# Hybrid backbone block on one core: one operand's low part by a VectorE subtraction, four weight sums on GpSimd

## The chip, the cores and the metric

The kernel runs on one core of a Trainium2 chip. The metric is the device time of one execution in microseconds (us), lower is better. Every execution computes both layers of the model from inputs in device memory. A difference of 0.2% (5.4 us) is about what repeated measurements of this kernel can tell from none.

## The reference

Two layers over 256 latent tokens and 256 context tokens of width 1024, all in fp32. Each layer is a half-step SwiGLU feed-forward network (FFN), a mixer with three branches, and a second FFN; each is modulated by a conditioning vector and closed by a layer norm. What matters here is the FFN, for the latent tokens `x` and the context tokens `xc` with the same weights:

```python
def swiglu(u, w1, w3, w2):
    return (jax.nn.silu(u @ w1) * (u @ w3)) @ w2

def ffn_sublayer(h, mod, w1, w3, w2, g, b):
    u = h * (1 + mod[1]) + mod[0]
    return layer_norm(ALPHA * h + 0.5 * mod[2] * swiglu(u, w1, w3, w2), g, b)

x = ffn_sublayer(x, ada_x[0], ffn_w1[l, 0], ffn_w3[l, 0], ffn_w2[l, 0], ...)
xc = ffn_sublayer(xc, ada_c[0], ffn_w1[l, 0], ffn_w3[l, 0], ffn_w2[l, 0], ...)
```

The hidden width is 2816, that is 22 tiles of 128 columns (`ft` 0 to 21).

## The kernel before

**Precision.** An fp32 product is made of three fp32r matmuls: every operand is split into a high part (a copy to fp32r on ScalarE, ACT) and a low part (operand minus high part, a subtraction on VectorE, DVE), and high x high, high x low and low x high are added up in PSUM. `split_into` (L228 to L230) writes such a pair for a weight or an activation, `wchunk` (L181) loads one weight tile of 512 KB into a buffer `raw` and splits it (L189, L190).

**Block products.** In the second FFN of layer 0 and the first of layer 1, hidden tiles 4 to 21 (18 in each, 36 in all) take the two weights' products with both token streams from seven block products instead of eight. `wquads` (L193) makes the weight side of one tile: it loads `r1` and `r3` (w1 and w3, L202), each with two halves of 512 columns for the two halves of the contraction, and makes four pairs:

- `a` (wahi, walo) from `r1`;
- `d` (wdhi, wdlo) from the second half of `r3`;
- then four sums of halves, written in place over `r3` and `r1` (L214 to L217, each reading what the one before it wrote);
- `c` (wchi, wclo) from the new `r1`, `b` (wbhi, wblo) from the new `r3`.

The low part of `b` is made in another way than the rest: ACT copies `b`'s high part with a sign change into it (L223), and a DMA issued from the GpSimd (POOL) queue adds `r3` to that (L224, an accumulating DMA).

**Order on TensorE (PE).** `block` (L255) runs 12 matmuls of 256 columns for one product: 4 blocks of the contraction, three matmuls each (L263 high, L264 high, L265 low). `issue_after` chains the blocks, so that PE takes them in program order. For hidden tile n the order is: two blocks with a(n); one with d(n-1), the tile before (`x_blocks`); one with c(n) (`third_block`); one with c(n-1) (`ctx_blocks`); two with b(n) (`last_blocks`): seven blocks, 84 matmuls. Between the blocks small activation steps run on ACT and DVE (L575 to L608): L575, L588 and L594 copy a product out of PSUM on ACT, L583, L595, L601, L606 and L608 combine on DVE, L584 and L607 are SiLU, and `store` splits the result (gh, gl).

**Buffers.** Pool `wp` has five buffers each for `raw` (NR), high parts (`hi`) and low parts (`lo`, NW). A tile needs four pairs, and two pairs of the tile before are still in use, so a pair waits until an earlier one is read out. Weight preparation is issued at a higher priority than its place in the program (`tc.high_priority`, PRE = 140); the framework's scheduler sets the order on each engine from that.

**Around it.** The tiles come in groups of 3, 8 and 7 in each of the two FFNs; between the groups the down projection runs (w2ps, L242 to L244). In the background, DVE computes the conditioning (`ada_job`, L289 and L291, one multiply-add over 512 columns each); `tick` in `wquads` and `wchunk` lets it advance by a fixed rate per weight tile.

Of the kernel before, what the change touches and what calls it, by code (L numbers as in the profile page):

```python
# [8 lines left out]
F32 = mybir.dt.float32  # L9
F32R = mybir.dt.float32r  # L10
AF = mybir.ActivationFunctionType
ALU = mybir.AluOpType
# [39 lines left out]
def hybrid_kernel(tc, x, ctx, pos, cc, wada, pcol, w1, w3, w2a, w2b, wst, wv, wg, wbr, wout, dfc, dft, idn, lnrow, out):  # L52
    nc = tc.nc
# [11 lines left out]
    def nm(s):  # L65
        cnt[0] += 1
        return f"{s}_{cnt[0]}"
# [32 lines left out]
    act = nc.scalar.activation  # L100
    V = nc.vector
# [74 lines left out]
    def tick():  # L176
        debt[0] += rate[0]
        n = int(debt[0])
        debt[0] -= n
        bg(n)  # L180
# [12 lines left out]
    def wquads(src1, src3):  # L193


        tick()
        H = slice(0, 512), slice(512, 1024)
        with tc.high_priority(offset=PRE):
            raw = []
            for src in (src1, src3):  # L200
                t = wp.tile([P, 1024], F32, tag="raw", bufs=NR, name=nm("raw"))
                nc.sync.dma_start(out=t, in_=src)  # L202
                raw.append(t)
            r1, r3 = raw

            def halves(name, w=1024):
                return [wp.tile([P, 1024], F32R, tag=t, bufs=NW, name=nm(name + t))[:, :w] for t in ("hi", "lo")]

            a = halves("wa")
            split_into(a[0], a[1], r1)  # L210
            d = halves("wd", 512)
            split_into(d[0], d[1], r3[:, H[1]])
            add = dict(op=ALU.add)
            V.tensor_tensor(r3[:, H[1]], r3[:, H[0]], r3[:, H[1]], **add)  # L214
            V.tensor_tensor(r3[:, H[0]], r3[:, H[0]], r1[:, H[0]], **add)
            V.tensor_tensor(r1[:, H[0]], r3[:, H[1]], r1[:, H[0]], **add)
            V.tensor_tensor(r1[:, H[1]], r1[:, H[0]], r1[:, H[1]], **add)  # L217
            c = halves("wc")
            split_into(c[0], c[1], r1)

            b = halves("wb")
            act(b[0], r3, AF.Copy)
            act(b[1], b[0].bitcast(F32), AF.Copy, scale=-1.0)  # L223
            nc.gpsimd.dma_start(out=b[1].bitcast(F32), in_=r3, accum_op=ALU.add)  # L224

        return (a, 0), (a, 512), (d, 0), (b, 512), (c, 0), (b, 0), (c, 512)

    def split_into(h, l, src):  # L228
        first = act(h, src, AF.Copy)  # L229
        return first, V.tensor_tensor(l, src, h.bitcast(F32), op=ALU.subtract)  # L230
# [304 lines left out]
    def ffn(l, i, X, ys, T, nxt):  # L535
# [32 lines left out]
        def start_blocks(ft):  # L568

            f = dict(ft=ft, W=wquads(w1[l, i, ft], w3[l, i, ft]))  # L570
            f["r1"] = bank(mmp, "q1")[:, XR]
            f["c"], f["v"] = aslot("cc"), aslot("cv", 256)
            Q[:] = X.operands()
            block(f["r1"], f["W"][0], Q[0], True)
            act(f["c"][:, XR], f["r1"], AF.Copy)  # L575
            return f
# [539 lines left out]
    for part in range(4):  # L1116
# [4 lines left out]
        for kt in range(0, KT, 2):  # L1121
            raw = wp.tile([P, 1024], F32, tag="raw", bufs=NR, name=nm("araw"))
            for k in range(2):
                nc.sync.dma_start(out=raw[:, 512 * k:512 * k + 512].rearrange("p (v c) -> p v c", v=2),
                                  in_=wada[0, (kt + k) * P:(kt + k + 1) * P, 0:2 * D]
# [189 lines left out]
```

## Time and profile before

| | us |
|---|---|
| median of 3 runs (2713.5 to 2718.81) | 2718.05 |
| the profiled execution | 2721.58 |
| its span, first to last instruction | 2719.8 |
| TensorE matmuls busy | 2538.8 (93%) |
| VectorE busy | 1966.5 (72%) |
| ScalarE busy | 1109.8 (41%) |
| GpSimd busy | 80.5 (3%) |
| mean granted TensorE clock | 0.967 of full speed |

Matmuls are pipelined: a matmul's busy time overlaps the next one's, so the distance between two starts says what one costs. A row of a timeline gives start, duration, engine (SPq and the like are DMA queues), line, operation, output <- inputs, and in brackets how long the engine sat idle before it and what ended that.

### The profile page before, as it was taken

To read this page: it belongs to the slowest core of one execution; us is meant where nothing else is said; L and a number is where in the kernel's file an instruction comes from. 1 tells how busy PE (TensorE), PEld (TensorE's weight loads), DVE (VectorE), ACT (ScalarE), POOL (GpSimd) and SP (SyncE) were. 2 spreads that over 40 slices of the span, in tenths; PEclk is the share of its full clock that TensorE was granted. 3 is DMA by queue.
4 is the path that set the end of the run, shared out by engine and by line. 5 is a ranking of instruction groups with operands and counts; after the bars stand their busy time and mean duration, and the time that the engine had idled before them with its cause. 6 is when DMAs were issued, how large, how long until landed. Compare 5 with 4: busy or idle time off the path is not lost. (4 is left out here: it accounts for less than half of the span.)

```text
span 2719.8 us, 40624 instructions
## 1 busy us (share of the span) xinstructions
PE 2538.8 (93%) x15842; PEld 2231.9 (82%) x15842; DVE 1966.5 (72%) x3611; ACT 1109.8 (41%) x1834; POOL 80.5 (3%) x162
## 2 busy tenths in 40 slices
PE   8999999999999999998879799878889999999998
PEld 4777779788778888897767788777779888999998
DVE  5888887888777755587666568656556988987655
ACT  4222235333332324353442446343445334455543
POOL 0000000010100000000000000000000000000000
PEclk9999999999999999998889899988899999999999
DMA  9666663222133233326454444546353333556563
GB/s 287 197 207 191 190 199 108 90 67 89 59 102 96 67 128 97 120 86 170 111 130 133 115 132 133 146 132 178 106 142 99 106 116 119 176 166 210 159 197 125
DMA packets 135744, 372.99 MB, mean 137 GB/s; under 512 B 13313, under 2 KB 28929, under 8 KB 135553
## 3 DMA queue, kind: packets, MB, share of 16 engines
q1 hardware_dynamic: 130368, 351.53, 41.4%
q0 software_dynamic: 5184, 18.88, 3.7%
q8 instruction: 124, 2.03, 0.3%
q14 instruction: 68, 0.55, 0.1%
HBM read 344.11 MB, written 7.34 MB: 129 GB/s over the span
## 5 line engine op out<-in xcount | busy, mean ns | idle before, releaser
L189 ACT ACTIVATE whi<-raw 128x1024 fp32r<-128x1024 f32 (+1 forms) x426 | 444.1, 1044 | 872.6 <-issue 170.1
L190 DVE TENSOR_TENSOR wlo<-raw,whi 128x1024 fp32r<-128x1024 f32 (+1 forms) x426 | 511.5, 1202 | 278.7 <-ACT whi L189 275.6
L673 DVE SCALAR_TENSOR_TENSOR cy<-cz,dww,cy 128x482 f32<-128x482 f32 (+29 forms) x480 | 288.9, 602 | 17.4 <-ACT cy L765 10.5
L291 DVE SCALAR_TENSOR_TENSOR acc<-araw,sc,acc 128x512 f32<-128x512 f32 x392 | 275.1, 746 | 18.2 <-DMA araw<-in_wada_dram 17.3
L265 PE MATMUL q<-tH,wblo 128*128 128x256 f32 x288 | 109.5, 380 | 113.9 <-DMA wblo<-raw 113.9
L265 PEld LDWEIGHTS q<-tH,wblo 128*128 128x128 f32 x288 | 79.0, 274 | 122.5 <-DMA wblo<-raw 122.5
L242 PE MATMUL ffps<-op,whi 128*128 128x256 f32 x608 | 165.3, 281 | 3.9 <-ACT op L229 3.9
L243 PE MATMUL ffps<-op,whi 128*128 128x256 f32 x608 | 168.1, 280 | 0.0
L244 PE MATMUL ffps<-op,wlo 128*128 128x256 f32 x608 | 167.5, 279 | 0.0
L242 PE MATMUL ffps<-opH,whi 128*128 128x512 f32 x352 | 141.0, 403 | 0.7 <-ACT opH L229 0.7
L243 PE MATMUL ffps<-opL,whi 128*128 128x512 f32 x352 | 140.7, 400 | 0.0
L244 PE MATMUL ffps<-opH,wlo 128*128 128x512 f32 x352 | 140.1, 400 | 0.4 <-DVE wlo L190 0.4
L242 PE MATMUL w2ps<-gh,whi 128*128 128x512 f32 x336 | 134.2, 399 | 0.0
L244 PE MATMUL w2ps<-gh,wlo 128*128 128x512 f32 x336 | 133.5, 397 | 0.0
L243 PE MATMUL w2ps<-gl,whi 128*128 128x512 f32 x336 | 133.1, 396 | 0.0
L242 PE MATMUL mg<-opH,whi 128*128 128x512 f32 (+1 forms) x384 | 129.7, 338 | 0.0
L244 PE MATMUL mg<-opH,wlo 128*128 128x512 f32 (+1 forms) x384 | 129.5, 337 | 0.0
L243 PE MATMUL mg<-opL,whi 128*128 128x512 f32 (+1 forms) x384 | 129.4, 337 | 0.0
L242 PEld LDWEIGHTS ffps<-op,whi 128*128 128x128 f32 x608 | 113.0, 190 | 4.8 <-ACT op L229 4.3
L243 PEld LDWEIGHTS ffps<-op,whi 128*128 128x128 f32 x608 | 115.1, 190 | 0.2
L244 PEld LDWEIGHTS ffps<-op,wlo 128*128 128x128 f32 x608 | 114.8, 189 | 0.0
L263 PE MATMUL q<-tH,wbhi 128*128 128x256 f32 x288 | 102.7, 357 | 0.0
(390 smaller groups left out, 7358.0 us busy)
## 6 DMA issues: line engine op xcount, KB each, us to landing
raw<-in_w_dram SPq DMA_DIRECT2D x176, 512.0 KB, 4.1
raw<-in_wst_dram SPq DMA_DIRECT2D x144, 512.0 KB, 3.5
araw<-in_wada_dram SPq DMA_DIRECT2D x128, 512.0 KB, 4.2
raw<-in_w2b_dram SPq DMA_DIRECT2D x64, 512.0 KB, 4.2
raw<-in_wbr_dram SPq DMA_DIRECT2D x48, 512.0 KB, 3.5
wblo<-raw POOLq DMA_DIRECT2D x36, 512.0 KB, 5.3
raw<-in_w2a_dram SPq DMA_DIRECT2D x32, 384.0 KB, 3.2
araw<-in_wada_dram SPq DMA_DIRECT2D x32, 256.0 KB, 5.7
```

What stands on the lines that cost most here:

```text
L189: act(hi, raw, AF.Copy)
L190: V.tensor_tensor(lo, raw, hi.bitcast(F32), op=ALU.subtract)
L242: PE.matmul(ps, wh, xh, start=first and i == 0, stop=False)
L243: PE.matmul(ps, wh, xl, start=False, stop=False)
L244: PE.matmul(ps, wl, xh, start=False, stop=last and i == n - 1)
L263: PE.matmul(ps, wh, xh, start=first and k == 0, stop=False, **how)
L265: end = PE.matmul(ps, wl, xh, start=False, stop=k == 3, **how)
L291: V.scalar_tensor_tensor(accs[s], w, c, accs[s], op0=ALU.mult, op1=ALU.add)
L673: V.scalar_tensor_tensor(dv[:, :, a:b], sv[:, :, a + o:b + o], wcols[:, j:j + 1], dv[:, :, a:b], op0=ALU.mult, op1=ALU.add)
```

## The change

The four sums move from VectorE to GpSimd. The low part of `b` is made by `split_into`, like that of `a`, `c` and `d`: a subtraction on VectorE in place of ScalarE's sign-changed copy and the accumulating DMA. In the changed file the lines after `wquads` stand three lower: L229 and L230 are L226 and L227, L575 is L572, and so on.

```diff
             add = dict(op=ALU.add)
-            V.tensor_tensor(r3[:, H[1]], r3[:, H[0]], r3[:, H[1]], **add)
-            V.tensor_tensor(r3[:, H[0]], r3[:, H[0]], r1[:, H[0]], **add)
-            V.tensor_tensor(r1[:, H[0]], r3[:, H[1]], r1[:, H[0]], **add)
-            V.tensor_tensor(r1[:, H[1]], r1[:, H[0]], r1[:, H[1]], **add)
+            nc.gpsimd.tensor_tensor(r3[:, H[1]], r3[:, H[0]], r3[:, H[1]], **add)
+            nc.gpsimd.tensor_tensor(r3[:, H[0]], r3[:, H[0]], r1[:, H[0]], **add)
+            nc.gpsimd.tensor_tensor(r1[:, H[0]], r3[:, H[1]], r1[:, H[0]], **add)
+            nc.gpsimd.tensor_tensor(r1[:, H[1]], r1[:, H[0]], r1[:, H[1]], **add)
             c = halves("wc")
             split_into(c[0], c[1], r1)
-
             b = halves("wb")
-            act(b[0], r3, AF.Copy)
-            act(b[1], b[0].bitcast(F32), AF.Copy, scale=-1.0)
-            nc.gpsimd.dma_start(out=b[1].bitcast(F32), in_=r3, accum_op=ALU.add)
+            split_into(b[0], b[1], r3)
```

Where the scheduler puts the instructions. First ScalarE, between two evacuations of b's product (cv) in the middle of a group of tiles; before:

```order
L594 ACTIVATE cv_11554<-q_1832_11552 128x256
L229 ACTIVATE wchi_11671<-raw_11655 128x1024
L575 ACTIVATE cc_11681<-q_1849_11680 128x256
L222 ACTIVATE wbhi_11675<-raw_11657 128x1024
L584 ACTIVATE cc_11681<-cc_11681 128x256
L223 ACTIVATE wblo_11676<-wbhi_11675 128x1024
L229 ACTIVATE wahi_11802<-raw_11798 128x1024
L588 ACTIVATE cc_11681<-q_1849_11680 128x256
L229 ACTIVATE wdhi_11806<-raw_11800 128x512
```

and the same stretch of the changed kernel:

```order
L591 ACTIVATE cv_11546<-q_1832_11544 128x256
L226 ACTIVATE wchi_11663<-raw_11647 128x1024
L572 ACTIVATE cc_11672<-q_1849_11671 128x256
L226 ACTIVATE wbhi_11667<-raw_11649 128x1024
L581 ACTIVATE cc_11672<-cc_11672 128x256
L226 ACTIVATE wahi_11793<-raw_11789 128x1024
L585 ACTIVATE cc_11672<-q_1849_11671 128x256
L226 ACTIVATE wdhi_11797<-raw_11791 128x512
```

One copy of 1024 columns is gone; all else stands as it stood, wchi ahead of the copy of a's product (cc).

VectorE in the same stretch of the changed kernel, from one wclo to the last step before the next:

```order
L227 TENSOR_TENSOR wclo_11664<-raw_11647,wchi_11663 128x1024
L580 TENSOR_TENSOR cc_11672<-q_1852_11687,cc_11672 128x256
L227 TENSOR_TENSOR wblo_11668<-raw_11649,wbhi_11667 128x1024
L598 SCALAR_TENSOR_TENSOR cc_11545<-q_1832_11544,cc_11545 128x256
L227 TENSOR_TENSOR walo_11794<-raw_11789,wahi_11793 128x1024
L603 TENSOR_TENSOR cc_11545<-q_1838_11620,cc_11545 128x256
L227 TENSOR_TENSOR wdlo_11798<-raw_11791,wdhi_11797 128x512
L605 SCALAR_TENSOR_TENSOR cc_11545<-cv_11546,cc_11545 128x256
L227 TENSOR_TENSOR gl_11744<-cc_11545,gh_11743 128x512
```

wblo (the third row) is new here; the four sums, which stood between wdlo and the next wclo, are gone from this engine. They stand on GpSimd, whose queue in this stretch was one accumulating DMA per tile and now is, for one tile:

```order
L214 TENSOR_TENSOR raw_11649<-raw_11649 128x512
L215 TENSOR_TENSOR raw_11649<-raw_11649,raw_11647 128x512
L216 TENSOR_TENSOR raw_11647<-raw_11649,raw_11647 128x512
L217 TENSOR_TENSOR raw_11647<-raw_11647 128x512
```

Nothing else of the block tiles moved onto that queue. PE's order of blocks and SP's order of loads are the same in both kernels.

## Rows read from the trace of the kernel before

**Rows 1.** Waits, the whole span: who waited for whom, total us, times, longest.

```profile
PE q L265 <- DMA wblo<-raw: 113.9, 36, 5.8
```

**Rows 2.** Timeline of ACT, one tile.

```profile
1338.98 1.05 ACT L229 ACTIVATE wchi<-raw 128x1024 fp32r<-128x1024 f32 x1
...
1341.10 1.06 ACT L223 ACTIVATE wblo<-wbhi 128x1024 fp32r<-128x1024 f32 x1
...
1344.05 0.63 ACT L229 ACTIVATE wdhi<-raw 128x512 fp32r<-128x512 f32 x1 [0.37 <-PE q L264]
```

**Rows 3.** Timeline of all engines: the same tile's accumulating DMA, and PE's wait.

```profile
1342.46 0.87 POOL L224 DMA_DIRECT2D wblo<-raw  x1 [16.25 <-ACT wblo L223]
...
1348.52 0.58 PE L265 MATMUL q<-tH,wblo 128*128 128x256 f32 x1 [4.16 <-DMA wblo<-raw]
```

**Rows 4.** Timeline of PE: starts at full clock, then at half.

```profile
1341.22 0.28 PE L263 MATMUL q<-tH,wchi 128*128 128x256 f32 x1
...
1343.97 0.28 PE L263 MATMUL q<-tH,wbhi 128*128 128x256 f32 x1
...
1353.59 0.41 PE L264 MATMUL q<-op,wahi 128*128 128x256 f32 x1
1353.80 0.41 PE L265 MATMUL q<-op,walo 128*128 128x256 f32 x1
```

**Rows 5.** Windows: us; busy us of PE, PEld, DVE, ACT, POOL; granted clock, DMA.

```profile
1347.70:1354.50 6.80, 5.99 (x28) 5.99 (x29) 2.74 (x6) 0.38 (x1) 0.00 (x0) 0.50 0.22 79
```

**Rows 6.** Timeline of PE: wblo waits that open and close the four long groups.

```profile
1314.77 0.58 PE L265 MATMUL q<-tH,wblo 128*128 128x256 f32 x1 [3.53 <-DMA wblo<-raw]
1426.73 0.58 PE L265 MATMUL q<-tH,wblo 128*128 128x256 f32 x1 [4.52 <-DMA wblo<-raw]
1487.31 0.38 PE L265 MATMUL q<-tH,wblo 128*128 128x256 f32 x1 [4.64 <-DMA wblo<-raw]
1572.74 0.39 PE L265 MATMUL q<-tH,wblo 128*128 128x256 f32 x1 [1.56 <-DMA wblo<-raw]
1762.28 0.39 PE L265 MATMUL q<-tH,wblo 128*128 128x256 f32 x1 [1.29 <-DMA wblo<-raw]
1870.00 0.58 PE L265 MATMUL q<-tH,wblo 128*128 128x256 f32 x1 [2.21 <-DMA wblo<-raw]
1928.79 0.58 PE L265 MATMUL q<-tH,wblo 128*128 128x256 f32 x1 [3.33 <-DMA wblo<-raw]
2021.18 0.38 PE L265 MATMUL q<-tH,wblo 128*128 128x256 f32 x1 [1.25 <-DMA wblo<-raw]
```

**Rows 7.** Timeline of DVE: starts of the steps of a tile.

```profile
1340.07 1.23 DVE L230 TENSOR_TENSOR wclo<-raw,wchi 128x1024 fp32r<-128x1024 f32 x1 [0.26 <-ACT wchi L229]
1341.21 0.42 DVE L583 TENSOR_TENSOR cc<-q,cc 128x256 f32<-128x256 f32 x1
1341.54 0.41 DVE L601 SCALAR_TENSOR_TENSOR cc<-q,cc 128x256 f32<-128x256 f32 x1
...
1344.29 0.75 DVE L291 SCALAR_TENSOR_TENSOR acc<-araw,sc,acc 128x512 f32<-128x512 f32 x1
1344.95 0.69 DVE L230 TENSOR_TENSOR wdlo<-raw,wdhi 128x512 fp32r<-128x512 f32 x1
```

**Rows 8.** Timeline of GpSimd: memsets of 128 and 512 columns, and hand-over between engines.

```profile
0.84 0.21 POOL L117 MEMSET onem<- 128x128 f32 x1
...
295.99 0.53 POOL L698 MEMSET RT<- 128x512 f32 x1 [294.12 <-PE w2ps L244]
...
1164.37 0.15 DVE L371 SCALAR_TENSOR_TENSOR lnred<-lnst,lnred 128x2 f32<-128x2 f32 x1
1164.69 0.69 POOL L373 TENSOR_TENSOR lnrr<-lnred,mhalf 128x2 f32<-128x2 f32 x1 [147.41 <-DVE lnred L371]
1165.42 0.16 DVE L377 SCALAR_TENSOR_TENSOR lnrr<-lnst,lnrr 128x2 f32<-128x2 f32 x1 [0.49 <-POOL lnrr L373]
```

**Rows 9.** One line's instructions (L850): duration in ns, min/median/max.

```profile
L850 POOL TENSOR_SCALAR_AFFINE_SELECT pm<-pm x48: 285/294/1181, 517.2 to 2281.8; 128x128 f32<-128x128 f32 x48
```

## The prediction

> **What bounds the kernel now.** I read the table first (matmuls on TensorE, PE, fill 93% of the span), then the waits, then timelines of one tile on each engine. Of PE's idle time the largest single cause is one wait in the 36 block tiles: [rows 1] show 113.9 us in 36 waits for the accumulating DMA that finishes wblo, 3.2 us each.
>
> One tile tells why it is late. ACT writes the negated copy into wblo from 1341.10 for 1.06 us [rows 2]; the DMA is issued from GpSimd (POOL) at 1342.46, and PE goes on at 1348.52 after 4.16 us of idling [rows 3], so the detour from the copy's end to PE costs 6.4 us. PE has only two blocks with c to do meanwhile.
>
> The wait has a second price. The 24 matmuls of two blocks start within 2.75 us, 0.114 us each, at full clock, and 0.21 us apart later in the same tile [rows 4]; the granted clock from 1347.7 to 1354.5 was 0.50, the lower of its two levels, 1.2 GHz [rows 5], and PE had been idle just before.
>
> What a tile takes altogether: between the first and the last wblo wait of the four long groups [rows 6] lie 112.0, 85.4, 107.7 and 92.4 us, for 7, 6, 7 and 6 tiles: 397.5 / 26 = **15.3 us** per tile. At full clock 84 matmuls at 0.114 need 9.6 us. So 5.7 us per tile are open: about 3.2 of waiting, the rest slow clock.
>
> **The change part by part.** *wblo by subtraction.* Removed per tile: ACT's copy (1.06 us), the DMA's issue, the DMA. Added: a DVE subtraction like wclo's, after which the next step starts 1.14 us later (1340.07 to 1341.21) [rows 7]. With the copy of a's product (L572) between wchi and wbhi, wbhi ends some 2.4 us after wchi's start, wblo some 3.8 us after it (4.4 with a background step, 0.66, ahead of it). PE may start c(n)'s block when wclo is there, at about 2.4, and wants wblo two blocks (2.7 us) later, at 5.1. The wait for wblo is gone: minus 3.2 us, and it takes its slow clock along. ACT's saved copy is worth nothing by itself: ACT is busy 41%.
>
> *The sums on GpSimd.* Four dependent additions. On DVE each stood between other steps and kept nobody waiting for long. The trace has no GpSimd addition over 512 columns, so I bound it. Below: a memset of 512 columns, which reads nothing, 0.53 us [rows 8]. A select of 128 columns, which reads and writes once, takes 0.29 us [rows 9], a memset of 128 columns 0.21 [rows 8]: a read stream costs about 0.08 us per 128 columns, 0.3 per 512, and two of them on the memset give 1.1 us. Four whole selects and one more read stream give 1.5. Above: the two-input power of 2 columns takes 0.69 us [rows 8]; if all of that is a fixed cost of two-input operations, 0.7 + 1.4 = 2.1 us. I take **1.3 us**, the middle of 1.1 and 1.5, since the select is the nearest row; 0.5 and 2.1 stay for the range.
>
> The Trainium skill's page "GPSIMD Engine Reference", section 3.1, puts a two-input addition on GpSimd at 4497 ns for 2048 fp32 columns. A quarter of it is an estimate of 1.12 us, at the low end of my two middle figures; by it a tile would be 0.7 us shorter than below and the kernel some 20 us faster. No run here shows it so far.
>
> *What is late next.* wchi waits for the last sum. The sums wait for wdlo, wdlo for wdhi, and wdhi takes the buffer that PE's block with c(n-1) frees (ACT idled 0.37 us for PE there [rows 2]). On DVE, whose queue is in order, wdlo stands behind wclo, L580, wblo, L598, walo and L603. This closes a loop from one tile's wchi to the next one's. Step by step, as distances between starts: wchi to wclo 1.09 [rows 2, 7]; wclo 1.14, wblo 1.14, walo 1.14; L580, L598 and L603 0.33 each [rows 7]; so wdlo starts at 5.5, ends at 6.2 (0.69), the first sum starts 0.17 later (DVE to POOL, [rows 8]) at 6.4. Four sums of 1.3 with 0.04 for each hand-over [rows 8]: 11.8. Background steps (L288): the changed order has about 0.6 per tile ahead of wdlo, 0.66 each: 12.2. PE then idles 2.6 us per tile ahead of c(n), somewhat less than now, so part of the slow clock stays; the stretch of the loop in which PE works, the two c blocks, runs from 2.4 to 4.9 at full clock, and L603 stands at 5.2, so 0.3 of a delay is free. A slow stretch like [rows 5] would add up to 2.5 us to the two blocks; one of half that length in most tiles adds about 0.8. **T = 13.0 us** per tile.
>
> *The sum.* 30 intervals between tiles of a group, 15.3 to 13.0: 69 us. For the six first tiles of groups nothing precedes in the loop; four of their waits are 3.53, 4.64, 1.29 and 3.33 us [rows 6], mean 3.2, six of them 19 us; I count 13 and leave 6 for a late c. Together 82 us: the profiled execution's 2721.6 becomes 2640. The median shown is 3.5 us below that execution, so **2636 us**, 3.0% less. DVE is relieved of four times 0.6 us of start-to-start time per tile and given 1.14; that has its effect in the loop above and counts nothing elsewhere, since outside the block tiles no instruction is changed.
>
> **The rivals.**
>
> *A: DVE and GpSimd slow each other.* If the two cannot read SBUF at the same time in two-input operations, the sums wait for DVE's. Between wdlo and wclo stand L605 (0.42), gl (0.69) and about 1.3 background steps (0.75): 2.1 us per tile, all of it on the loop at worst. T becomes 13.0 + 1.3 to 2.1, say 14.5, and the gain 0.8 x 30 + 10 = 34 us: 2684. Against it: half of these would run in gaps of the chain. In the trace before the two engines hardly ever work at once, so no row decides. The Trainium skill's page "SBUF — State Buffer", section "Who interferes with whom", has this as a rule: a DVE instruction with two SBUF inputs and a GpSimd instruction that reads SBUF exclude each other for their whole length. No row before shows or refutes it. Chance 0.27.
>
> *B: the sums are cheap.* At 0.8 us each (between the memset and the 1.1), the loop is 12.2 - 2.0 = 10.2 us, PE idles 0.6 per tile, too little to lose the clock (the three waits under 1.6 us in [rows 6] were each followed by a matmul of 0.38 or 0.39 us, not the 0.58 of the slow ones, though one long wait was too). Gain 5.1 x 30 + 16 = 169: 2549. For it: nothing but the lower bound. Chance 0.13.
>
> *C: slower.* One mechanism: ACT's wchi, and PE's block with c behind it, wait for the four sums longer than PE now waits for the DMA. It decides from 15.3 us per tile, that is from a sum of 1.3 + 2.3 / 4 = 1.9 us. At the upper bound, 2.1, T is 16.2, 30 tiles lose 27 us and the first tiles win 13: 2732. For it: [rows 8], the long power operation, and rival A may come on top. Against it: the select of 128 columns takes 0.29, no fixed cost of 0.7. Chance 0.11.
>
> *D: no change.* wblo waits for DVE as long as it waited for the DMA. That needs 5 us of other work ahead of it in DVE's queue; the order has at most two background steps there. Chance 0.02.
>
> **How the numbers follow.** My forecast has 0.47, with a range of its own from 2600 to 2668 (a sum of 1.0 to 1.55 us). The range for 8 in 10 reaches into A up to 2700 and into B down to 2565; it leaves out C, D's like and the better part of B. Faster by over 0.2% (5.4 us, what repeated measurements can tell): forecast, A and B, 0.87. Slower: C, 0.10. Within 0.2%: 0.03.
>
> **What would show it.** Right: no waits of PE for a DMA into wblo; in their place waits of PE for wclo or for ACT's wchi, 2 to 3 us per tile, ACT's wchi waiting for GpSimd's L217, four additions of 1.1 to 1.5 us each in a row on GpSimd, tiles some 13 us apart, and a granted clock that still falls in part of the tiles. Wrong by A: L605, gl and L288 on DVE, or the sums, longer beside each other than alone (0.42, 0.69, 0.75). Wrong by B: PE waits under 1 us. Wrong by C: sums near 2 us and tiles over 15 us apart. If PE still waits for wblo, my reading of DVE's queue is wrong.

## The result, and the profile after

The changed kernel takes **2678.51 us** (median of 3 runs, 2673.11 to 2679.18) against 2718.05: 0.984 of the time before, 95% interval 0.981 to 0.988, 39.5 us less. The forecast was 2636 us; the time lies in the range (2565 to 2700), outside the forecast's own range (2600 to 2668), and next to rival A's 2684.

The page of the changed kernel: busy time of each engine, and TensorE's granted clock in 40 slices.

```profile
PE 2531.9 (95%) x15842; PEld 2223.9 (83%) x15842; DVE 1974.7 (74%) x3503; ACT 1075.1 (40%) x1798; POOL 258.1 (10%) x270
...
PEclk9999999999999999999989999989999999999999
```

GpSimd's busy time has risen from 80.5 to 258.1 us. VectorE is busier than before (1966.5), although 144 sums have left it and only 36 subtractions came: that is the first sign that something lasts longer there.

The waits, and from the answer on the tile wblo the line on who waited for it; these answer to [rows 1].

```profile
ACT wchi L226 <- POOL raw L217: 162.9, 35, 7.0
DVE wclo L227 <- ACT wchi L226: 90.2, 32, 6.3
PE q L260 <- ACT cc L572: 61.9, 28, 7.2
```

```profile
  PE q L262: 1.8, 1
```

The wait of 113.9 us for the DMA is gone; for wblo PE waits once, 1.8 us. In its place PE waits 61.9 us ahead of c(n). The row names the copy L572, which stands behind wchi in ACT's queue [see the order of ACT ahead of the prediction], and wchi waits 162.9 us for the last sum, as the prediction's loop has it.

One tile, answering to [rows 7]. GpSimd's timeline:

```profile
1314.13 1.41 POOL L214 TENSOR_TENSOR raw<-raw 128x512 f32<-128x512 f32 x1 [10.50 <-DMA raw<-in_w_dram]
1315.62 1.62 POOL L215 TENSOR_TENSOR raw<-raw,raw 128x512 f32<-128x512 f32 x1
1317.32 1.59 POOL L216 TENSOR_TENSOR raw<-raw,raw 128x512 f32<-128x512 f32 x1
1318.99 1.26 POOL L217 TENSOR_TENSOR raw<-raw 128x512 f32<-128x512 f32 x1
```

and VectorE's beside it, with PE's wait after it:

```profile
1313.37 0.68 DVE L227 TENSOR_TENSOR wdlo<-raw,wdhi 128x512 fp32r<-128x512 f32 x1
1313.97 0.42 DVE L605 SCALAR_TENSOR_TENSOR cc<-cv,cc 128x256 f32<-128x256 f32 x1
1314.31 1.78 DVE L288 SCALAR_TENSOR_TENSOR acc<-araw,sc,acc 128x512 f32<-128x512 f32 x1
1316.01 1.77 DVE L227 TENSOR_TENSOR gl<-cc,gh 128x512 fp32r<-128x512 f32 x1
1317.71 0.41 DVE L592 TENSOR_TENSOR cv<-q,cv 128x256 f32<-128x256 f32 x1
1321.37 1.23 DVE L227 TENSOR_TENSOR wclo<-raw,wchi 128x1024 fp32r<-128x1024 f32 x1 [3.25 <-ACT wchi L226]
```

```profile
1321.66 0.58 PE L260 MATMUL q<-tH,wchi 128*128 128x256 f32 x1 [3.76 <-ACT cc L572]
```

Read the two engines against each other. L288 and gl, 0.75 and 0.69 us long in the kernel before, take 1.78 and 1.77; each starts inside a sum and ends 0.5 to 0.6 us after it. The next sum starts before that and takes 1.6 us instead of 1.26. L592, whose first operand lies in PSUM, takes its usual 0.41 beside a sum. L217, with nothing beside it, takes 1.26. Over all tiles (duration in ns, min/median/max):

```profile
L214 POOL TENSOR_TENSOR raw<-raw x36: 1285/1409/1715, 1222.7 to 1964.0; 128x512 f32<-128x512 f32 x36
...
L215 POOL TENSOR_TENSOR raw<-raw,raw x36: 1277/1618/1628, 1224.1 to 1965.5; 128x512 f32<-128x512 f32 x36
...
L216 POOL TENSOR_TENSOR raw<-raw,raw x36: 1262/1354/1758, 1225.8 to 1967.2; 128x512 f32<-128x512 f32 x36
...
L217 POOL TENSOR_TENSOR raw<-raw x36: 1259/1307/1627, 1227.5 to 1968.5; 128x512 f32<-128x512 f32 x36
```

The loop of the prediction, step by step. The measured column is the mean over the 30 intervals between tiles of a group, each a distance between starts (or from the last sum's end) in the timelines of ACT, DVE and GpSimd.

| step of a tile | forecast, us | measured, us |
|---|---|---|
| wchi to wclo | 1.09 | 1.14 |
| wclo to the next wdlo | 5.6 (4.4, background 0.4, slow clock 0.8) | 6.17 |
| wdlo to the first sum | 0.86 | 0.77 |
| four sums | 5.3 | 6.07 |
| last sum to wchi | 0.04 | 0.07 |
| tile (T) | 13.0 | 14.2 |

By the same measure the kernel before has 15.2. Inside the groups the change gains 454.9 - 426.4 = 28.5 us (69 forecast), outside them some 15 (13 forecast); the two profiled spans differ by 43.2.

The second row of the table holds the slow clock. Windows from wclo to the next wdlo of five successive tiles of one group (us; busy us of PE, PEld, DVE, ACT, POOL; granted clock, DMA):

```profile
1478.58:1483.22 4.64, 3.86 (x31) 3.66 (x32) 4.55 (x6) 3.48 (x7) 0.00 (x0) 1.00 0.50 129
1490.94:1496.99 6.05, 5.27 (x31) 5.07 (x32) 4.64 (x7) 3.60 (x7) 0.00 (x0) 0.72 0.51 169
1504.66:1513.06 8.40, 8.21 (x58) 8.22 (x59) 5.56 (x14) 3.99 (x8) 0.00 (x0) 0.80 0.40 125
1520.78:1527.04 6.26, 5.48 (x31) 5.28 (x32) 4.64 (x7) 3.60 (x7) 0.00 (x0) 0.73 0.51 158
1534.76:1541.01 6.25, 5.47 (x31) 5.26 (x32) 4.64 (x7) 3.60 (x7) 0.00 (x0) 0.73 0.54 156
```

The same 31 matmuls take 3.86 us at a granted clock of 1.00 and 5.3 to 5.5 at 0.72 to 0.73, where part of the stretch ran at the lower level; the stretch grows from 4.64 to 6.05 to 6.26 us with them.

The window of 8.40 us is of another kind. A small transposition for the conditioning (L298) stands in PE's order inside the first block with a. It waits for a copy on ACT (L296), and that copy stands behind wchi in ACT's queue:

```profile
1504.54 0.26 ACT L296 ACTIVATE adar<-adaps 128x128 f32<-128x128 f32 x1
1504.85 0.33 PE L298 MATMUL adat<-ident,adar 128*128 128x128 f32 x1 [3.68 <-ACT adar L296]
```

So here PE waits for the last sum before it has finished with a, and the rest of a's blocks and the block with d, 26 matmuls, come after the wait and ahead of c(n). Three of the 30 tiles are such: PE waits 3.0 to 3.9 us ahead of the transposition (at most 0.9 in the kernel before), and they take 16.1 to 17.2 us. The other 27 take 13.9 on average, and their second row is 5.87.

### The profile page after: what moved, and what is told of

It is laid out like the page before. It is cut to its first block, busy times and chain, and to the rows that moved or that the text cites. A ratio compares the mean times of both kernels' runs of the same rounds, so it can differ in the third digit from the quotient of the medians.

```text
span 2676.6 us, 40594 instructions
## 1 busy us (share of the span) xinstructions
PE 2531.9 (95%) x15842; PEld 2223.9 (83%) x15842; DVE 1974.7 (74%) x3503; ACT 1075.1 (40%) x1798; POOL 258.1 (10%) x270
## 4 chain that ended last, share of the span: by engine, by line
PE 56%; DVE 13%; issue 13%; DMA 7%; POOL 7%; ACT 2%; SPq 0%; POOLq 0%; DVEq 0%; ACTq 0%
DMA raw<-in_w_dram 5%; DVE acc L288 3%; DVE wlo L190 3%; PE ffps L239 3%; PE br L239 2%; PE br L240 2%; PE ffps L240 2%; PE ffps L241 2%; PE br L241 2%; PE mg L239 2%; PE mg L241 2%; PE mg L240 2%; PE clo L239 2%; PE clo L240 2%; PE clo L241 2%
## 5 line engine op out<-in xcount | busy, mean ns | idle before, releaser
L288 DVE SCALAR_TENSOR_TENSOR acc<-araw,sc,acc 128x512 f32<-128x512 f32 x392 | 308.6, 833 | 23.8 <-DMA araw<-in_wada_dram 23.2
L227 DVE TENSOR_TENSOR wclo<-raw,wchi 128x1024 fp32r<-128x1024 f32 x36 | 44.1, 1224 | 90.2 <-ACT wchi L226 90.2
L260 PE MATMUL q<-tH,wchi 128*128 128x256 f32 x144 | 51.2, 356 | 61.9 <-ACT cc L572 61.9
L226 ACT ACTIVATE wchi<-raw 128x1024 fp32r<-128x1024 f32 x36 | 38.0, 1057 | 162.9 <-POOL raw L217 162.9
```

Of the source, the lines that this page charges most:

```text
L260: PE.matmul(ps, wh, xh, start=first and k == 0, stop=False, **how)
L288: V.scalar_tensor_tensor(accs[s], w, c, accs[s], op0=ALU.mult, op1=ALU.add)
```

## The experiments

| kernel | median, us | ratio to before, 95% interval | tile, us | granted clock over the block tiles |
|---|---|---|---|---|
| before | 2718.05 | 1 | 15.2 | 0.91 |
| the change | 2678.51 | 0.984 (0.981 to 0.988) | 14.2 | 0.94 |
| e1_low_only | 2567.01 | 0.944 (0.942 to 0.946) | 11.1 | 0.99 |
| e2_sums_only | 2728.28 | 1.003 (1.001 to 1.005) | 15.3 | 0.90 |
| e3_one_sum_dve | 2652.41 | 0.975 (0.973 to 0.977) | 13.6 | 0.95 |
| e4_no_sums | 2547.28 | 0.935 (0.933 to 0.938) | 10.8 | 0.99 |
| e5_sums_twice | 2883.96 (one run) | - | 20.0 | 0.83 |
| e7_fill | 2776.6 | 1.021 (1.019 to 1.023) | 17.2 | 0.93 |
| e8_fill_free | 2697.9 | 0.994 (0.993 to 0.996) | 15.3 | 0.96 |

The tile is the mean distance from one wchi to the next over the same 30 intervals; medians of before in the experiments' own runs were 2723.2, 2719.5 and 2714.5 us.

**e1_low_only**: the first half of the change alone.

```diff
-            nc.gpsimd.tensor_tensor(r3[:, H[1]], r3[:, H[0]], r3[:, H[1]], **add)
+            V.tensor_tensor(r3[:, H[1]], r3[:, H[0]], r3[:, H[1]], **add)
...
```

(all four sums so, against the changed kernel)

> Half of the change: b's low part by a VectorE subtraction, the four sums stay on VectorE. Loop theory (a tile takes as long as the loop wchi, wclo, PE's two c blocks, wdhi, wdlo, four sums, wchi): the sums take 0.6 us each from start to start instead of 1.3 to 1.6, the loop falls to about 10.5 us, close to the 9.6 us that PE's matmuls need, the granted clock no longer falls in most tiles; 30 x (15.2 - 10.5) + 16 = 157 us less than before, about 2560 us. Rival 'VectorE's queue is the bound': four more subtractions and sums in one queue give 12 us per tile, 2610 us. Rival 'the wait only moves': 2690 us or more.

Measured 2567 us, 7 us from the loop theory's figure; tiles 11.1 us (means of the four long groups 10.7 to 11.3), where 10.5 was expected. That the time came so near is luck in part: inside the groups this version gains 121 us where the expectation has 141, outside them 33 where it has 16. VectorE's timeline from wdlo to the last sum, in a tile without background work:

```profile
1445.93 0.69 DVE L227 TENSOR_TENSOR wdlo<-raw,wdhi 128x512 fp32r<-128x512 f32 x1
1446.54 0.42 DVE L605 SCALAR_TENSOR_TENSOR cc<-cv,cc 128x256 f32<-128x256 f32 x1
1446.87 0.68 DVE L214 TENSOR_TENSOR raw<-raw 128x512 f32<-128x512 f32 x1
...
1449.74 0.68 DVE L217 TENSOR_TENSOR raw<-raw 128x512 f32<-128x512 f32 x1
...
1451.61 1.23 DVE L227 TENSOR_TENSOR wclo<-raw,wchi 128x1024 fp32r<-128x1024 f32 x1 [0.30 <-ACT wchi L226]
```

The four sums with two other steps between them span 3.55 us (1446.87 to 1450.42), 3.7 on average over all tiles, against 6.07 on GpSimd, and the granted clock over the block tiles is 0.99:

```profile
1225.00:1890.00 665.00, 637.24 (x4619) 585.03 (x4619) 556.59 (x932) 309.28 (x505) 2.46 (x4) 0.99 0.44 139
```

PE is busy 96% of that window, VectorE 84%: the rival of VectorE's queue as the bound falls for most tiles. This version beats both kernels.

**e2_sums_only**: the second half alone, the sums on GpSimd and b's low part as before.

```diff
-            V.tensor_tensor(r3[:, H[1]], r3[:, H[0]], r3[:, H[1]], **add)
+            nc.gpsimd.tensor_tensor(r3[:, H[1]], r3[:, H[0]], r3[:, H[1]], **add)
...
```

(all four, against the kernel before)

> The other half: the sums on GpSimd, b's low part still by ScalarE's copy and the accumulating DMA. Loop theory: PE's wait for the DMA into wblo stays and sets the tile (15 to 16 us), the longer loop of 14 us lies beside it; c may come late as well in some tiles: 2710 to 2745 us. Rival 'the sums on GpSimd relieve VectorE and that is what the change gained': 2680 to 2690 us, as with the whole change.

Measured 2728 us, 0.3% above before, which is also how far the medians of before lie apart. The wait for the DMA stands as it stood in [rows 1], and in some tiles wchi waits for the sums as well:

```profile
PE q L265 <- DMA wblo<-raw: 113.0, 35, 8.0
...
ACT wchi L229 <- POOL raw L217: 49.6, 10, 6.9
```

So the sums' move gained nothing by itself. Put on top of the other half it costs 2678.5 - 2567.0 = 111 us: the whole gain of the change, and 111 us more, is in the subtraction.

**e3_one_sum_dve**: the whole change with one sum back.

```diff
-            nc.gpsimd.tensor_tensor(r3[:, H[0]], r3[:, H[0]], r1[:, H[0]], **add)
+            V.tensor_tensor(r3[:, H[0]], r3[:, H[0]], r1[:, H[0]], **add)
```

> The whole change, but the second sum (b's first half, which the later sums need only to have read its operand) back on VectorE. Loop theory: the chain of sums falls from 6.1 to about 5 us, tiles from 14.2 to about 13 us with less slow clock, 30 to 45 us less than the whole change: about 2640 us. Rival 'what bounds is the sum of the times in which VectorE's two-input steps and GpSimd exclude each other': 0.6 us more on VectorE, 1.3 less on GpSimd, at most 0.7 us per tile: 2660 us. Rival 'GpSimd's chain is hidden': no change, 2678 us.

Measured 2652 us, tiles 13.6. GpSimd's timeline of one tile:

```profile
1342.21 1.41 POOL L214 TENSOR_TENSOR raw<-raw 128x512 f32<-128x512 f32 x1 [7.68 <-DVE wdlo L227]
1344.85 1.68 POOL L216 TENSOR_TENSOR raw<-raw,raw 128x512 f32<-128x512 f32 x1 [1.23 <-DVE raw L215]
1346.60 1.59 POOL L217 TENSOR_TENSOR raw<-raw 128x512 f32<-128x512 f32 x1
```

The middle sum takes 1.23 us of GpSimd's waiting in place of the 1.7 it took there: it stands behind a background step on VectorE (L288, 1.78 us there) that L214 holds up. The chain's mean is 5.7 us, not the 5.0 expected, and the gain lies between the loop's figure and that of the rival of mutual exclusion (2660). The two aren't told apart by this run: both act in the same chain.

**e4_no_sums**: the four sums left out.

```diff
-            nc.gpsimd.tensor_tensor(r3[:, H[1]], r3[:, H[0]], r3[:, H[1]], **add)
...
```

> The whole change without the four sums (they are left out: b and c are made from the unsummed weights). Loop theory: wchi no longer waits for GpSimd, the loop falls below PE's own 9.6 us, PE becomes the bound at full clock: tiles of 9.7 to 10 us, about 2540 us. Rival 'VectorE is the bound even so': 11 us or more per tile, over 2580 us. Rival 'the slow clock stays whatever the waits': 2600 us.

Measured 2547 us, near the 2540 expected. The tiles take 9.7 to 10.1 us on average in the long groups (the 10.8 of the table holds two of 24.2 and 18.2 us in the short ones), and PE is busy 99% of the stretch:

```profile
1209.00:1850.00 641.00, 632.84 (x4685) 588.85 (x4685) 478.24 (x797) 312.05 (x507) 2.46 (x4) 0.99 0.46 142
```

With PE that full, little is left to gain in this order of blocks: e1 is 20 us from it, with the sums.

**e5_sums_twice**: every sum made twice.

```diff
             nc.gpsimd.tensor_tensor(r3[:, H[1]], r3[:, H[0]], r3[:, H[1]], **add)
+            nc.gpsimd.tensor_tensor(r3[:, H[1]], r3[:, H[0]], r3[:, H[1]], **add)
...
```

> The whole change with each of the four sums made twice (the second time adds again, so c and b are other weights). Loop theory: nothing hides the chain, four more additions of 1.26 to 1.4 us with their hand-over lengthen every tile by 5.4 to 6 us, and more slow clock comes with it: 2678 + 30 x 5.4 to 6.5, 2840 to 2870 us. Rival 'part of the chain lies beside PE's blocks': under 2800 us.

Measured 2884 us, one run, 14 us above the range expected; tiles 20.0 us, 5.8 more. Four more sums in a tile last 5.4 to 5.7 us with their hand-overs, so none of the added chain is hidden; the stretch from wclo to the next wdlo, with a granted clock of 0.83 over the block tiles, grows by 0.3. That is 30 x 5.8 = 174 of the 205 us more; the rest lies between the groups. The wait stands where the loop puts it (L221 is the last sum, L264 the first matmul of c(n) there):

```profile
ACT wchi L230 <- POOL raw L221: 315.3, 36, 12.9
...
PE q L264 <- ACT wchi L230: 198.4, 28, 8.5
```

**e6_probe**: the disputed cost by itself, behind the last step of the changed kernel: `p`, `q`, `x`, `y` are tiles of 512 columns in SBUF, `ps` one in PSUM.

```diff
     ffn(1, 1, U, ys, TX, None)
+    for n in range(6):
+        G.tensor_tensor(p, p, q, **add)
...
+    for n in range(8):
+        V.tensor_tensor(x, x, y, **add)
...
+    for n in range(10):
+        V.tensor_tensor(x, ps, x, **add)
...
+    for n in range(8):
+        V.tensor_scalar(x, x, 0.5, None, op0=ALU.mult)
```

(the six additions on GpSimd stand beside each of the loops on VectorE)

> The whole change, and behind the kernel's last step four stretches of six dependent GpSimd additions of 512 columns: alone; beside eight VectorE additions with two SBUF inputs; beside ten with one PSUM and one SBUF input; beside eight VectorE multiplications by a constant (one SBUF input). Theory 'two-input steps on VectorE and GpSimd additions exclude each other': alone 1.26 us each and no more beside the PSUM kind; in the second stretch the additions take 1.6 us or more from start to start and VectorE's rise from 0.68 to about 1.8; in the fourth, from the changed kernel's one step of 0.48 us that took 1.6, the same. Rival 'whatever VectorE does slows GpSimd': the second, third and fourth stretch alike. Rival 'the tiles' longer additions come from DMA traffic': all stretches 1.26 us. The time of this run is longer by the probe itself, some 40 us, and tells nothing.

GpSimd's additions alone, then beside each kind of VectorE step, with that step below it (duration in ns, min/median/max):

```profile
L1186 POOL TENSOR_TENSOR pp<-pp,pq x6: 1262/1262/1782, 2674.2 to 2681.5; 128x512 f32<-128x512 f32 x6
...
L1189 POOL TENSOR_TENSOR pp<-pp,pq x6: 1588/1588/1765, 2683.5 to 2692.0; 128x512 f32<-128x512 f32 x6
L1191 DVE TENSOR_TENSOR px<-px,py x8: 692/1632/1632, 2683.5 to 2694.2; 128x512 f32<-128x512 f32 x8
...
L1195 POOL TENSOR_TENSOR pp<-pp,pq x6: 1262/1263/1266, 2697.1 to 2703.8; 128x512 f32<-128x512 f32 x6
L1197 DVE TENSOR_TENSOR px<-pps,px x10: 691/691/692, 2697.1 to 2703.6; 128x512 f32<-128x512 f32 x10
...
L1201 POOL TENSOR_TENSOR pp<-pp,pq x6: 1322/1324/1497, 2707.2 to 2714.4; 128x512 f32<-128x512 f32 x6
L1203 DVE TENSOR_SCALAR px<-px x8: 426/1366/1368, 2707.2 to 2716.1; 128x512 f32<-128x512 f32 x8
```

An addition on GpSimd takes 1.26 us alone. Beside VectorE steps with two SBUF inputs it takes 1.59, and theirs go from 0.69 to 1.63. With one input in PSUM neither changes. The multiplication by a constant, with one SBUF input, suffers as well (0.43 to 1.37), the additions beside it little (1.32). Both rivals fall. The theory is right on which steps hold each other up, and too strong on how much: a round of one two-input addition on each engine takes 1.67 us (GpSimd's second and third start at 2685.37 and 2687.04), where the two alone add up to 1.95, so they overlap by some 0.3 us. VectorE's additions were expected at 1.8 us and took 1.63; beside the multiplications GpSimd was expected at 1.6 and took 1.32.

**e7_fill and e8_fill_free**: unread matmuls in PE's wait, to keep its clock up. e7 writes them to the bank of the second product (q2) of the same tile, e8 to that of the third (q3) of the tile before. The lines of e7; in e8 the call stands behind `x_blocks` and takes the tile before:

```diff
+        def fill(f, n=20):
+            with tc.issue_after(blocks_end[-1].ins):
+                for _ in range(n):
+                    end = PE.matmul(f["fill"][:, CR], identr, Q[0][0][0], start=True, stop=True)
+            blocks_end[:] = [end]
...
                     x_blocks(open_[0])
+                fill(f)
                 third_block(f)
```

> The whole change, and ahead of each c(n) block 20 matmuls of 256 columns whose result nobody reads (2.3 us at full clock), in the place where PE waits. Theory 'the slow clock after the wait is part of the loop': the granted clock stays high, the stretch from wclo to the next wdlo falls from 6.2 to about 4.7 us, tiles from 14.2 to about 12.9 us: 2635 us. Rival 'PE's two c blocks have slack against VectorE's queue': no change, 2675 us or, where the filling outlasts the wait, up to 2690 us.

> As e7_fill, but the 20 unread matmuls write to the PSUM bank of the tile before, whose last reader stands ahead of wclo on VectorE, so that they run in PE's wait and not behind it (in e7_fill they waited for VectorE's L581 and ran after the wait: 17 us per tile). Theory 'the slow clock after the wait is part of the loop': granted clock near 1.0 in the block tiles, wclo to wdlo 4.7 us instead of 6.2, tiles 12.7 to 13 us, 2630 to 2645 us. Rival 'the two c blocks have slack': the clock rises and the tile stays at 14.2 us, 2678 us. Rival 'the clock falls for another reason': clock and time as in the whole change.

e7 was a faulty test, and told something else. Its filling waited for VectorE's L581, the reader of q2's other half, which stands behind wclo:

```profile
1337.19 3.08 PE L587 MATMUL q<-op,identr 128*128 128x256 f32 x17 [3.76 <-DVE cc L581]
```

The matmuls came after the wait, not in it, and the time rose by 98 us over the change, 2.7 us in each of the 36 tiles; neither expectation had that. So PE's blocks with c are on the loop without slack.

In e8 (whose filling opens a new accumulation in a bank with unfinished sums, and so alters part of a tile's third product) the filling ran in the wait in most tiles. Windows from wclo to the next wdlo, the same group as above:

```profile
1476.01:1480.66 4.65, 4.49 (x39) 4.29 (x38) 4.55 (x7) 3.48 (x7) 0.00 (x0) 1.00 0.51 145
1488.40:1493.07 4.67, 4.50 (x39) 4.29 (x38) 4.56 (x7) 3.49 (x7) 0.00 (x0) 1.00 0.42 127
1500.75:1512.56 11.81, 11.63 (x78) 11.63 (x79) 5.66 (x14) 3.99 (x8) 0.00 (x0) 0.76 0.26 90
1520.30:1524.95 4.65, 4.65 (x41) 4.49 (x40) 4.56 (x6) 3.49 (x7) 0.00 (x0) 1.00 0.47 143
1532.69:1537.42 4.73, 4.55 (x39) 4.35 (x38) 4.60 (x7) 3.49 (x7) 0.00 (x0) 1.00 0.46 139
```

Where the clock stayed at 1.00 the stretch is 4.65 to 4.73 us, and those tiles took 12.4: 1.4 to 1.6 us less than the same three tiles of the change. But the whole took 2698 us, slower than the change; none of the three expectations came. In three tiles, the third row above among them, PE stood 3.8 to 5.1 us ahead of the transposition L298, and the filling came after that wait. And the scheduler set the background steps otherwise: in eleven tiles one stood ahead of wdlo and waited for its load, as here:

```profile
1325.51 0.75 DVE L288 SCALAR_TENSOR_TENSOR acc<-araw,sc,acc 128x512 f32<-128x512 f32 x1 [3.56 <-DMA araw<-in_wada_dram]
```

The clock's part in a tile is shown by these windows; what it would give over the whole kernel isn't.

## Why the prediction came out as it did

*The wait and its removal: right.* PE's wait for wblo went from 113.9 us to 1.8, with wblo on time in VectorE's queue. Rival D fell with that.

*What is late next: right.* The loop through wchi, the c blocks, wdlo and the sums is in the waits, in the table of its steps, and in e4 and e5, which take its chain away and double it, with 2547 us where 2540 was expected and 2884 where 2840 to 2870 was. One link was off: I had VectorE's queue ahead of wdlo a little longer than PE's two blocks. In the tiles at full clock wdhi starts 5.1 us after wchi and wdlo 0.66 after it, so PE's blocks lead there, and slow clock in them is paid in full.

*The sums' own price: right, with some luck.* 1.3 us was taken, 1.26 measured alone, far from both bounds. It was the middle of 1.1 and 1.5, with the select as the reason; but the select gave the 1.5, and 1.26 lies nearer to the 1.1 from the memset. A quarter of the Trainium skill's figure for 2048 columns ("GPSIMD Engine Reference", section 3.1), an estimate of 1.12 us, is 11% below it.

*The steps that failed are two terms of the sum.* The four sums in a row took 6.07 us instead of 5.3, because VectorE's L605, gl and background steps stand in the same stretch and the engines hold each other up; the forecast had priced the sums as if alone. The chain is 5.8 us in the tiles without a background step beside it and 6.2 on average in those with two. And the stretch from wclo to wdlo took 6.17 instead of 5.6. Of these 0.57 us, 0.24 are its bottom, 4.64 us at full clock without background work where I had 4.4, and 0.30 are the three tiles in which PE stands ahead of the transposition, a wait that the prediction doesn't have. In the other 27, slow clock and background work come to 1.23 us, and I had 1.2. Per tile that is 1.2 us in all, 30 x 1.2 = 36 of the 42 us by which the time missed the forecast; 4 more lie in the base, 15.3 by wblo's waits where wchi to wchi gives 15.2.

*Rival A was what happened*, with its mechanism and place shown in the probe and the timelines: I had it at 0.27 and at 14.5 us per tile, it came out at 14.2. That its 2684 us lie so near is luck in part. I had put 1.3 to 2.1 us on the loop for it; the chain grew by only 0.75, because what VectorE loses there (gl and L288 at twice their length) falls into its own wait for wclo, and the rest of the 1.2 us is the other term above.

The prediction says that no row before decides on A. That was a misreading of [rows 9], where the longest select takes 1181 ns at a median of 294. Four of the 48 selects began while a VectorE step with both operands in SBUF ran; they took 0.73 to 1.18 us and ended 0.15 us after that step. The other 44 took 0.29 to 0.30, most of them beside VectorE steps with an operand in PSUM. One of the four, in the kernel before:

```profile
2279.85 1.22 DVE L190 TENSOR_TENSOR wlo<-raw,whi 128x1024 fp32r<-128x1024 f32 x1
2280.23 0.99 POOL L850 TENSOR_SCALAR_AFFINE_SELECT pm<-pm 128x128 f32<-128x128 f32 x1 [6.71 <-ACT pm L847]
```

So the trace showed GpSimd waiting for such a step, and A deserved a higher chance than 0.27. By the Trainium skill's rule ("SBUF — State Buffer", section "Who interferes with whom") I would have made A the forecast: the probe agrees with it on which steps contend, 1.59 and 1.63 us with two SBUF inputs, 1.26 and 0.69 with one of them in PSUM, and 1.37 for a constant multiplication in SBUF, one of the operations that the page lists. It doesn't bear out that the two exclude each other for their whole length, as the prediction gave the rule: a round takes 1.67 us and not 1.95.

*Rival B* (cheap sums) fell with the 1.26 us. *Rival C* fell too: 14.2 us stay below the 15.3 at which it decides; 1.26 and even 1.6 are below the 1.9 it needed. e2 comes nearest to it, 0.3% slower, by the sums without the subtraction.

What stays open: what the exclusion alone is worth in time. No run takes it away and leaves the chain; its 0.75 us per tile is read from the chain's length.

## What to carry to other kernels

Follow the wait that a change removes to the loop that then closes, and price every link of it; the engine that was relieved may not be in that loop. Work moved to an idle engine costs its full price there if it is a link: in this loop the four sums span 3.7 us on VectorE (e1) and 6.07 on GpSimd. A longest duration far above the median, as in [rows 9], is worth a look at what ran beside it. Where a change has two halves, time them apart: one was worth 5.6%, the other gave most of it back.

## What the runs showed of the hardware

- Two-input additions on GpSimd (128 x 512, fp32) take 1.26 us alone, 1.26 to 1.76 in the kernel (medians of the four 1.31 to 1.62); a dependent one starts 0.07 to 0.08 us after the end of the one before.
- VectorE's steps pay more than GpSimd's in that contention: 0.69 to 1.63 us against 1.26 to 1.59 in the probe. A round of one of each takes 1.67 us, 0.3 less than the two alone together. VectorE's additions with one operand in PSUM pay nothing (0.69 us).
- After 21 of TensorE's 28 waits ahead of c(n) in the change (0.9 to 7.2 us) the mean granted clock over the 4 us from its end was 0.50 to 0.77, after the other seven 1.00. The wait's length alone doesn't decide it: after 1.42 and 1.79 us the clock fell, after 1.87 and 1.94 it didn't. At 11.1 us per tile, in e1, the granted clock over the block tiles was 0.99.
